# The last head's attention output in two halves: two PSUM banks, matmuls in order of readiness, one half scaled on ScalarE

## The chip, the cores and the metric

The kernel runs on one core of a Trainium2 chip. The metric is the device time of one execution in microseconds (us). The profile's span is the part of it between the first and the last instruction, here 1.7 to 3.0 us shorter, mostly 1.7 to 1.9. A transfer's issue is the instruction that starts it; its landing is the moment when its semaphore reports it complete. In the lines of the profile PE is TensorE, DVE is VectorE, ACT is ScalarE, POOL is GpSimd, and SPq and ACTq are the queues of the sync engine and of ScalarE, which issue the transfers here.

## The reference

Attention with an additive bias, for 4 x 8 heads, 1024 positions and head size 64, all in float32:

```
scores = q @ k^T / sqrt(64) + bias                    # bias [1, 1, 1024, 1024]
attn   = exp(scores - max) / (sum(exp(scores - max)) + 1e-8)
out    = attn @ v
```

## The kernel before

The heads are worked in 16 pairs. Scores are made transposed, 128 keys by 512 queries at a time; one such piece is a **block**, and there are 512 of them. For each block TensorE makes the scores, ScalarE takes the exponential (three blocks an instruction), VectorE multiplies by a table of exp(bias), and TensorE multiplies by V, to which a column of ones is appended, so that the 65th column is the sum of the weights. Eight blocks, one for each 128 keys, add up to the output of one head and 512 queries. They accumulate in one PSUM bank (PSUM is the memory of the tiles `ps_x` and `ps_s` in the code); then VectorE takes the reciprocal of the sums and scales.

The last eight blocks, 504 to 511, belong to the last head's second half of the queries. Blocks 510 and 511 are special: their bias is added in PSUM before the exponential, so they need no multiply. The Python program holds a list scheduler that decides the order of instructions on each engine when the program is built.

```python
    late_bias = {NB - 2: 0, NB - 1: 1}                 # NB = 512
    ...
    def av_bank(b, tag):                               # one block's 4 matmuls with V
        pr, h, qh, kc = banks[b]
        if kc == 0:
            po[h] = ps_x.tile([P, QC, D1], F32, tag=tag, name="po")
        acc = po[h]
        e = e_at(b, 1)
        for i in range(QC):                            # QC = 4 chunks of 128 queries
            nc.tensor.matmul(acc[:, i, :], e[:, 0, i * P:(i + 1) * P], vall[:, 2 * pr + h, kc, :],
                             start=(kc == 0 and i == 0), stop=(kc == NCH - 1), skip_group_check=True)
        if kc < NCH - 1:
            return None
        def evac():
            ...
            nc.vector.reciprocal(rs[:], acc[:, :, D:D1])
            c0 = qh * QC
            if b == NB - 1:                            # the very last one: two scalings, two transfers
                m = QC // 2
                for i, q in ((0, nc.sync), (m, nc.scalar)):
                    nc.vector.tensor_tensor(oall[:, c0 + i:c0 + i + m, :], acc[:, i:i + m, :D],
                                            rs[:, i:i + m, :].to_broadcast([P, m, D]), op=ALU.mult)
                    q.dma_start(out=of[2 * pr + h][:, c0 + i:c0 + i + m, :], in_=oall[:, c0 + i:c0 + i + m, :])
                return
            ...
    # order of the blocks on TensorE, last 16: as numbered
                av_order += list(range(u, NB))
```

The softmax here doesn't subtract the row's maximum and nothing guards it: scores larger than these inputs give would overflow.

Of the kernel before, what the change touches and what calls it, by code (L numbers as in the profile page):

```python
# [8 lines left out]
F32 = mybir.dt.float32  # L9
BF = mybir.dt.bfloat16  # L10
ACTF = mybir.ActivationFunctionType
ALU = mybir.AluOpType
# [3 lines left out]
def kernel(  # L16
# [15 lines left out]
    nc = tc.nc  # L32
    B, H, S, D = q.shape
    P = 128
    NCH = S // P
    D1 = D + 1
    NP = B * H // 2
    scale = 1.0 / (D ** 0.5)
    HQ = S // 2
    QC = NCH // 2  # L40
# [4 lines left out]
    of = out.rearrange("b h (p c) d -> (b h) p c d", p=P)  # L45
# [6 lines left out]
    op = ctx.enter_context(tc.tile_pool(name="op", bufs=2))  # L52
    small = ctx.enter_context(tc.tile_pool(name="small", bufs=4))
    ps_s = ctx.enter_context(tc.tile_pool(name="ps_s", bufs=2, space=bass.MemoryType.PSUM))
    ps_x = ctx.enter_context(tc.tile_pool(name="ps_x", bufs=1, space=bass.MemoryType.PSUM))
# [7 lines left out]
    vall = consts.tile([P, 2 * NP, NCH, D1], BF)  # L63
# [42 lines left out]
    banks = [(pr, h, qh, kc) for pr in range(NP) for qh in range(2) for kc in range(NCH) for h in range(2)]  # L106
    NB = len(banks)
# [8 lines left out]
    def e_at(b, n):  # L116
        if b // ET not in etiles:
            etiles[b // ET] = ep.tile([P, ET, HQ], BF, name="E")
        return etiles[b // ET][:, b % ET:b % ET + n, :]
# [57 lines left out]
    po = {}  # L177

    def av_bank(b, tag):
# [5 lines that stand above are left out]
        for i in range(QC):  # L185
# [6 lines that stand above are left out]
            if qh == 0:  # L192
                oalls[h] = op.tile([P, NCH, D], F32, tag=f"o{h}", name="oall")
            oall = oalls[h]
            rs = small.tile([P, QC, 1], F32, name="rs")
            nc.vector.reciprocal(rs[:], acc[:, :, D:D1])  # L196
            c0 = qh * QC
            if b == NB - 1:

                m = QC // 2  # L200
                for i, q in ((0, nc.sync), (m, nc.scalar)):
                    nc.vector.tensor_tensor(oall[:, c0 + i:c0 + i + m, :], acc[:, i:i + m, :D],
                                            rs[:, i:i + m, :].to_broadcast([P, m, D]), op=ALU.mult)
                    q.dma_start(out=of[2 * pr + h][:, c0 + i:c0 + i + m, :], in_=oall[:, c0 + i:c0 + i + m, :])
                return
            nc.vector.tensor_tensor(oall[:, c0:c0 + QC, :], acc[:, :, :D],  # L206
                                    rs[:].to_broadcast([P, QC, D]), op=ALU.mult)
            if pr == NP - 1:
                nc.sync.dma_start(out=of[2 * pr + h][:, c0:c0 + QC, :], in_=oall[:, c0:c0 + QC, :])
            elif qh == 1:  # L210
                nc.sync.dma_start(out=of[2 * pr + h], in_=oall[:])
        return evac

    with tc.manual_schedule():
# [97 lines left out]
        for u in range(0, NB, 16):  # L312
            if u + 16 < NB:
                av_order += [u + 2 * i for i in range(8)] + [u + 2 * i + 1 for i in range(8)]
            else:
                av_order += list(range(u, NB))
        av_next = 0

        def unit_of(b):
            return banks[b][:3]  # L320
# [44 lines left out]
        def pe_piece():  # L365
            if not pieces:
                return None
            pr, which, half = pieces[0]
            if pr not in raw_at or (pr < NP and pr not in raws):
                return None  # L370
            i = min(len(filled), NO - 1)
            while order[i][0] != "S":
                i -= 1
            at = slots[order[i][1]][0]
            if at < (pr - 2) * 32 + 8:
                return None

            left = NCH - av_next % NCH
            busy = x_unit.get(unit_of(av_order[av_next])) if av_next % NCH else None
            tags = sorted((x_free[x], x) for x in x_free if x != busy)  # L380
            if busy and left < 4 and at < pr * 32 - 16:
                return None
            if not busy and av_next and at < pr * 32 - 16 and tags[0][0] + SEM < t_pe and len(tags) > 1 and tags[1][0] > t_pe:
                return None
            free, tag = tags[0]
            ready = max(free + SEM, raw_at[pr][1 - which])

            def emit(t):
                pieces.pop(0)
                copy = transpose_pe(pr, which, half, tag) if pr < NP else late_bias_pe(tag)  # L390
                cost = COPYK if which else COPYQ
                x_free[tag] = 1e12

                def run(t2):
                    copy()
                    if (pr, which, half) == (0, 1, 1):
                        for x in range(2):
                            for y in range(2):
                                nc.vector.memset(mask[x * D:(x + 1) * D, y, :], 1.0 if x == y else 0.0)
                    x_free[tag] = t2 + cost  # L400
                    piece_end[(pr, which, half)] = t2 + cost
                    if pr < NP and which == 0 and half == 1:
                        if pr + 3 < NP:
                            load_qk(pr + 3)
                            raw_at[pr + 3] = (t2 + 7000, t2 + 7000)
                        if pr + 2 < NP:
                            load_v(pr + 2)
                dve_q.append((t + pe_cost(t, TP) + SEM, 0, cost, run))
            return ready, TP, emit

        def pe_av():
            if av_next >= NB:
                return None
            b = av_order[av_next]
            if b not in mul_at:
                return None
            ready = mul_at[b] + SEM
            u = unit_of(b)
            if banks[b][3] == 0:
                free, tag = min((x_free[x], x) for x in x_free)  # L420
                ready = max(ready, free + SEM)
            else:
                tag = x_unit[u]

            def emit(t):
                nonlocal av_next
                x_unit[u] = tag
                x_free[tag] = 1e12
                evac = av_bank(b, tag)
                av_next += 1  # L430
                if evac:
                    def run(t2):
                        evac()
                        x_free[tag] = t2 + EVAC
                    dve_q.append((t + AV + SEM, 3 if u == (NP - 1, 0, 1) else 1, EVAC, run))
            return ready, AV, emit
# [54 lines left out]
                return None  # L491
            return max(t_act, filled[i] + SEM), cost_act(i), i

        while len(act_end) < NO or av_next < NB or dve_q:
            c = []
            a, d, p = act_pick(), dve_pick(), pe_pick()
            if a:
                c.append((a[0], 0))
            if d:
                c.append((max(t_dve, d[0]), 1))  # L500
            if p:
                c.append((p[0], 2))
            if not c:
                p = pe_pick(force=True)
                c.append((p[0], 2))
            t, who = min(c)
            if who == 0:
                i = a[2]
                item = order[i]
                t_act = t + a[1]  # L510
                act_end.append(t_act)
                if item[0] == "S":
                    s_exp(item[1])
                    for b in slots[item[1]]:
                        exp_at[b] = t_act
                        if b in late_bias:
                            mul_at[b] = t_act
                else:
                    b_exp(item[1], item[2])
                    for kc in range(4):  # L520
                        eb_at[(item[1], item[2] + kc)] = t_act
            elif who == 1:
                if d in dve_q:
                    dve_q.remove(d)
                t_dve = t + d[2]
                d[3](t)
            else:
                t_pe = t + pe_cost(t, p[1])
                p[2](t)
# [30 lines left out]
```

## Time and profile before

| kernel before | |
|---|---|
| time, median of 6 runs | 251.45 us (250.32 to 252.20) |
| span of the profiled run | 249.37 us |
| ScalarE busy | 239.1 us, 96% of the span |
| start of the last-but-one multiply | 243.49 us |
| issue of the last output transfer | 246.28 us |

What the change can touch begins with the last-but-one multiply of VectorE, so I call its start **T** and give the times of the tail from T. They are taken from the trace's records, which are in nanoseconds. The lines of the page and of the tail are shown with the prediction.

### The profile page before, as it was taken

How to read it: one execution, taken by the hardware profiler on the slowest of the kernel's cores; microseconds unless marked ns; L12 is line 12 of the kernel's file. 1: busy time of each engine (PE TensorE's matmuls, PEld its weight loads, DVE VectorE, ACT ScalarE, POOL GpSimd, SP SyncE). 2: the span in 40 equal slices, each digit the busy share in tenths (PEclk: the TensorE clock that was granted, in tenths of full speed). 3: DMA queues.
4: the chain of work that ended last, by engine and by line, in shares of the span. 5: the costliest groups of instructions: out<-in, count | busy, mean ns of one | idle time of the engine just before them, and what ended most of it. 6: DMA issues, size and time to landing. Idle time of an engine off the chain costs nothing.

```text
span 249.4 us, 7121 instructions
## 1 busy us (share of the span) xinstructions
PE 228.1 (91%) x3096; PEld 141.6 (57%) x3151; DVE 220.5 (88%) x384; ACT 239.1 (96%) x181; POOL 52.6 (21%) x72
## 2 busy tenths in 40 slices
PE   6869999999999999999999999999999999999893
PEld 2346656656655655556566555566565555665552
DVE  3619799999999999999999999999999999988884
ACT  3799999999999999999999999999999999999991
POOL 6562315303113132204150130416000000000000
PEclk9999999999999999999999999999999999999998
DMA  8899999942923986923957194939901102020112
GB/s 145 171 206 184 192 122 164 122 94 45 169 45 71 108 112 113 113 87 49 165 82 89 47 117 93 121 95 113 111 34 43 45 0 88 3 84 3 63 45 64
DMA packets 48175, 23.79 MB, mean 95 GB/s; under 512 B 34448, under 2 KB 44048, under 8 KB 47888
## 3 DMA queue, kind: packets, MB, share of 16 engines
q0 software_dynamic: 42272, 14.42, 53.1%
q1 hardware_dynamic: 5312, 8.59, 9.6%
q8 instruction: 24, 0.39, 0.6%
q10 hardware_dynamic: 560, 0.33, 0.5%
q14 instruction: 7, 0.06, 0.1%
HBM read 29.36 MB, written 8.39 MB: 151 GB/s over the span
## 4 chain that ended last, share of the span: by engine, by line
ACT 82%; PE 10%; DVE 3%; issue 2%; DMA 2%; SPq 0%; DVEq 0%; ACTq 0%
ACT E L136 79%; PE ps L129 7%; ACT eb L149 3%; PE po L186 2%; DMA q0f<-in_q_dram 2%; PE px L89 1%; DVE E L161 1%; DVE E L155 1%; DVE oall L206 0%; DVE qT L98 0%; PE pq L250 0%; DVE rs L196 0%; PE px L245 0%; SPq L216 0%; ACT qr L260 0%
## 5 line engine op out<-in xcount | busy, mean ns | idle before, releaser
L136 ACT ACTIVATE E<-ps 128x1536 bf16<-128x1536 f32 (+2 forms) x172 | 230.1, 1681 | 2.0 <-PE ps L129 1.9
L129 PE MATMUL ps<-qT,kT 128*128 128x512 bf16 x457 | 135.3, 381 | 11.3 <-ACT E L136 4.8
L186 PEld LDWEIGHTS <-E 128*128 128x128 bf16 x2048 | 83.2, 98 | 38.8 <-DVE E L158 2.2
L158 DVE TENSOR_TENSOR E<-E,eb 128x2048 bf16<-128x2048 bf16 x78 | 94.1, 1217 | 7.6 <-ACT eb L149 6.4
L186 PE MATMUL po<-vall,E 128*128 128x65 bf16 x2048 | 92.9, 194 | 1.8 <-DVE E L158 0.5
L129 PEld LDWEIGHTS <-kT 128*128 128x128 bf16 x512 | 45.6, 97 | 43.1 <-issue 8.1
L161 DVE TENSOR_TENSOR E<-E,eb 128x1024 bf16<-128x1024 bf16 x92 | 61.0, 682 | 0.9 <-ACT E L136 0.7
L81 POOL DMA_DIRECT2D vall<-in_v_dram x32 | 28.1, 883 | 8.2 <-DVE vall L277 3.9
L75 POOL DMA_DIRECT2D kr<-in_k_dram x15 | 10.5, 700 | 87.6 <-PE px L89 86.3
L206 DVE TENSOR_TENSOR oall<-po,rs 128x256 f32<-128x256 f32 x63 | 26.7, 424 | 2.2
L98 DVE TENSOR_TENSOR qT<-px,mask 128x1024 bf16<-128x1024 bf16 x31 | 21.3, 687 | 2.8 <-PE px L89 1.9
L76 POOL DMA_DIRECT2D qr<-in_q_dram x15 | 10.8, 717 | 25.0 <-PE px L89 23.8
L102 DVE COPY kT<-px 128x512 bf16<-128x512 bf16 x31 | 13.1, 421 | 3.2 <-PE px L89 3.1
L196 DVE RECIPROCAL rs<-po 128x4 f32<-128x4 f32 x64 | 11.3, 176 | 2.6 <-PE po L186 2.2
L89 PE MATMUL px<-ident,qr 128*64 128x128 bf16 x248 | 12.8, 225 | 0.1
L89 PE MATMUL px<-ident,kr 128*64 128x128 bf16 x248 | 12.8, 224 | 0.1
L89 PEld LDWEIGHTS <-qr 128*64 128x64 bf16 x248 | 7.9, 109 | 8.6 <-issue 8.1
L89 PEld LDWEIGHTS <-kr 128*64 128x64 bf16 x248 | 7.9, 109 | 5.6 <-issue 3.6
L149 ACT ACTIVATE eb<-pb 128x2048 bf16<-128x2048 bf16 x4 | 7.5, 1878 | 0.0
L144 PE MATMUL pb<-ident,btraw 128*128 128x128 bf16 x64 | 4.6, 225 | 1.7 <-ACT eb L149 1.2
L144 PEld LDWEIGHTS <-btraw 128*128 128x128 bf16 x64 | 4.5, 147 | 2.5 <-issue 2.2
L155 DVE TENSOR_TENSOR E<-E,eb 128x1024 bf16<-128x1024 bf16 (+1 forms) x6 | 4.6, 774 | 0.6 <-ACT E L136 0.6
(41 smaller groups left out, 21.0 us busy)
## 6 DMA issues: line engine op xcount, KB each, us to landing
out_dram<-oall SPq DMA_DIRECT2D x30, 256.0 KB, 2.0
vall<-in_v_dram POOLq DMA_DIRECT2D x32, 128.0 KB, 5.8
kr<-in_k_dram POOLq DMA_DIRECT2D x15, 256.0 KB, 3.9
qr<-in_q_dram POOLq DMA_DIRECT2D x15, 256.0 KB, 4.5
btraw<-in_bias_dram POOLq DMA_DIRECT2D x2, 1024.0 KB, 10.9
out_dram<-oall SPq DMA_DIRECT2D x3, 128.0 KB, 1.7
q0f<-in_q_dram ACTq DMA_DIRECT2D x1, 128.0 KB, 2.5
k0f<-in_k_dram SPq DMA_DIRECT2D x1, 128.0 KB, 2.8
```

The source lines that it names most:

```text
L81: nc.gpsimd.dma_start(out=vall[:, 2 * pr + t, :, :D], in_=vf[pr, :, t])
L89: nc.tensor.transpose(px[t * D:(t + 1) * D, c, :], src[:, t, half * QC + c, :], ident[:])
L98: nc.vector.tensor_tensor(dst[:, :, half * HQ:(half + 1) * HQ], px.rearrange("p c q -> p (c q)").unsqueeze(1).to_broadcast([P, 2, HQ]), ma ...
L102: nc.vector.tensor_copy(dst[:, half * QC:(half + 1) * QC, :], px[:])
L129: nc.tensor.matmul(ps[:, j, :], kT[:, kc, :], qT[:, h, qh * HQ:(qh + 1) * HQ], start=True, stop=b not in late_bias)
L136: nc.scalar.activation(e_at(slots[g][0], n), open_ps.pop(("S", g))[:, :n, :], ACTF.Exp, scale=scale)
L149: nc.scalar.activation(eb[:, qh, k0:k0 + 4, :], open_ps.pop(("B", qh, k0))[:, :4, :], ACTF.Exp)
L158: nc.vector.tensor_tensor(e, e, eb[:, qh, kc:kc + 2, :].unsqueeze(2).to_broadcast([P, 2, 2, HQ]), op=ALU.mult)
L161: nc.vector.tensor_tensor(e, e, eb[:, qh, kc:kc + 1, :].to_broadcast([P, n, HQ]), op=ALU.mult)
L186: nc.tensor.matmul(acc[:, i, :], e[:, 0, i * P:(i + 1) * P], vall[:, 2 * pr + h, kc, :], start=(kc == 0 and i == 0), stop=(kc == NCH - 1), ...
L196: nc.vector.reciprocal(rs[:], acc[:, :, D:D1])
L206: nc.vector.tensor_tensor(oall[:, c0:c0 + QC, :], acc[:, :, :D], rs[:].to_broadcast([P, QC, D]), op=ALU.mult)
```

## The change

Its intent is a shorter tail. The last head's four chunks are split into two halves of two. Each half has a PSUM bank of its own, so that ScalarE, idle by then, can scale half 0 while VectorE scales half 1. And TensorE takes the blocks in order of readiness: 510 and 511, which need no multiply, go before 508 and 509.

```diff
+    def av_last(x, bs, tag):                       # half x, blocks bs
+        ...
+            po[x] = (ps_x if tag != "s" else ps_s).tile([P, M, D1], F32, tag=tag, name="po")
+        for i in range(M):                         # M = QC // 2 = 2
+            for b in bs:
+                nc.tensor.matmul(acc[:, i, :], e_at(b, 1)[:, 0, (x * M + i) * P:(x * M + i + 1) * P],
+                                 vall[:, 2 * NP - 1, banks[b][3], :], start=..., stop=..., skip_group_check=True)
+        ...
+            nc.vector.reciprocal(rs[:], acc[:, :, D:D1])
+            q = (nc.scalar, nc.sync)[x]
+            if x == 0:
+                for i in range(M):
+                    nc.scalar.activation(oh[:, i, :], acc[:, i, :D], ACTF.Copy, scale=rs[:, i, :])
+            else:
+                nc.vector.tensor_tensor(oh[:], acc[:, :, :D], rs[:].to_broadcast([P, M, D]), op=ALU.mult)
+            q.dma_start(out=of[2 * NP - 1][:, QC + x * M:QC + (x + 1) * M, :], in_=oh[:])
...
-                av_order += list(range(u, NB))
+                av_order += list(range(u, NB - 8))
...
+        def pe_last():                             # scheduler: of both halves, the step that is ready first;
+            ...                                    # 508 and 509 together, and last
```

More of the change, by code (lines that the diff above doesn't have):

```diff
@@ L197, in evac @@
             c0 = qh * QC
-            if b == NB - 1:
-                m = QC // 2
-                for i, q in ((0, nc.sync), (m, nc.scalar)):
-                    nc.vector.tensor_tensor(oall[:, c0 + i:c0 + i + m, :], acc[:, i:i + m, :D],
-                                            rs[:, i:i + m, :].to_broadcast([P, m, D]), op=ALU.mult)
-                    q.dma_start(out=of[2 * pr + h][:, c0 + i:c0 + i + m, :], in_=oall[:, c0 + i:c0 + i + m, :])
-                return
             nc.vector.tensor_tensor(oall[:, c0:c0 + QC, :], acc[:, :, :D],
@@ L211, in evac @@
                 nc.sync.dma_start(out=of[2 * pr + h], in_=oall[:])
+        return evac
+    M = QC // 2
+    last_left = [list(range(NB - 8, NB)) for _ in range(2)]
+    def av_last(x, bs, tag):
+        first = len(last_left[x]) == 8
+        if first:
+            po[x] = (ps_x if tag != "s" else ps_s).tile([P, M, D1], F32, tag=tag, name="po")
+        acc = po[x]
+        for b in bs:
+            last_left[x].remove(b)
+        for i in range(M):
+            for b in bs:
+                nc.tensor.matmul(acc[:, i, :], e_at(b, 1)[:, 0, (x * M + i) * P:(x * M + i + 1) * P],
+                                 vall[:, 2 * NP - 1, banks[b][3], :], start=first and i == 0 and b == bs[0],
+                                 stop=not last_left[x] and b == bs[-1], skip_group_check=True)
+        if last_left[x]:
+            return None
+        def evac():
+            oh = small.tile([P, M, D], F32, name=f"oh{x}")
+            rs = small.tile([P, M, 1], F32, name=f"rh{x}")
+            nc.vector.reciprocal(rs[:], acc[:, :, D:D1])
[6 more added lines that the diff above has]
+            q.dma_start(out=of[2 * NP - 1][:, QC + x * M:QC + (x + 1) * M, :], in_=oh[:])
         return evac
@@ L315 @@
             else:
-                av_order += list(range(u, NB))
+                av_order += list(range(u, NB - 8))
         av_next = 0
+        NA = len(av_order)
         def unit_of(b):
@@ L378, in pe_piece @@
             left = NCH - av_next % NCH
-            busy = x_unit.get(unit_of(av_order[av_next])) if av_next % NCH else None
+            busy = x_unit.get(unit_of(av_order[av_next])) if av_next < NA and av_next % NCH else None
             tags = sorted((x_free[x], x) for x in x_free if x != busy)
@@ L409, in pe_piece, with emit @@
             return ready, TP, emit
+        last_tag = [None, None]
+        def pe_last():
+            best = None
+            for x in range(2):
+                left = last_left[x]
+                if not left or (x == 1 and last_tag[0] is None):
+                    continue
+                steps = [[b] for b in left if b not in (NB - 4, NB - 3)] or [[NB - 4, NB - 3]]
+                for bs in steps:
+                    if any(b not in mul_at for b in bs):
+                        continue
+                    ready = max(mul_at[b] for b in bs) + SEM
+                    tag = last_tag[x]
+                    if tag is None and x == 0:
+                        free, tag = min((x_free[y], y) for y in x_free)
+                        ready = max(ready, free + SEM)
+                    elif tag is None:
+                        if len(act_end) < NO - 1 or len(filled) < NO:
+                            continue
+                        tag = "s"
+                        ready = max(ready, act_end[NO - 2] + SEM)
+                    c = (max(ready, t_pe), x, bs, tag)
+                    if best is None or c[0] < best[0]:
+                        best = c
+            if best is None:
+                return None
+            ready, x, bs, tag = best
+            cost = len(bs) * AV // 2
+            def emit(t):
+                if last_tag[x] is None and x == 0:
+                    x_free[tag] = 1e12
+                last_tag[x] = tag
+                evac = av_last(x, bs, tag)
+                if evac:
+                    dve_q.append((t + cost + SEM, 1, EVAC, lambda t2: evac()))
+            return ready, cost, emit
         def pe_av():
-            if av_next >= NB:
-                return None
+            if av_next >= NA:
+                return pe_last()
             b = av_order[av_next]
@@ L492, in act_pick @@
             return max(t_act, filled[i] + SEM), cost_act(i), i
-        while len(act_end) < NO or av_next < NB or dve_q:
+        while len(act_end) < NO or av_next < NA or any(last_left) or dve_q:
             c = []
```

## The prediction

> **What bounds the kernel now.** I read the page's engine shares first, then the chain that ended last for the whole span and again for its last few microseconds, and then the timeline of those microseconds, because the diff touches nothing earlier.
>
> ```profile
> PE 228.1 (91%) x3096; PEld 141.6 (57%) x3151; DVE 220.5 (88%) x384; ACT 239.1 (96%) x181; POOL 52.6 (21%) x72
> ACT 82%; PE 10%; DVE 3%; issue 2%; DMA 2%; SPq 0%; DVEq 0%; ACTq 0%
> ```
>
> ScalarE's exponentials set the pace: 239.1 of 249.4 us busy and 82% of the chain. The change adds and removes no exponential. What it can move is the tail behind the last one. The chain for 243 us to the end:
>
> ```profile
> 242.11 1.35 ACT E L136
> 243.47 0.02 issue
> 243.49 1.31 DVE E L155 x2
> 244.79 0.05 issue
> 244.84 0.68 PE po L186 x16
> 245.52 0.02 issue
> 245.54 0.19 DVE rs L196
> 245.74 0.02 issue
> 245.76 0.29 DVE oall L202
> 246.05 0.20 DVEq L555
> ```
>
> So the tail hangs not on the last exponential but on the one before it: that ends at 243.47, then two multiplies with the bias table run on VectorE (banks 506/507, then 508/509 of the 512 score blocks), then 16 matmuls, a reciprocal and the scaling. The timeline gives the neighbours:
>
> ```profile
> 243.22 1.15 ACT L136 ACTIVATE E<-ps 128x1024 bf16<-128x1024 f32 x1
> 244.24 0.42 PE L186 MATMUL po<-vall,E 128*128 128x65 bf16 x8 [0.19 <-DVE E L155]
> 244.70 0.17 DVE L196 RECIPROCAL rs<-po 128x4 f32<-128x4 f32 x1
> 244.84 0.67 PE L186 MATMUL po<-vall,E 128*128 128x65 bf16 x16 [0.18 <-DVE E L155]
> 244.91 0.42 DVE L206 TENSOR_TENSOR oall<-po,rs 128x256 f32<-128x256 f32 x1
> 245.54 0.18 DVE L196 RECIPROCAL rs<-po 128x4 f32<-128x4 f32 x1 [0.21 <-PE po L186]
> 245.76 0.49 DVE L202 TENSOR_TENSOR oall<-po,rs 128x128 f32<-128x128 f32 x2
> 246.08 0.33 SPq L204 DMA_DIRECT2D out_dram<-oall  x1
> 246.28 0.36 ACTq L204 DMA_DIRECT2D out_dram<-oall  x1
> ```
>
> Three things are to be seen. The last exponential (two blocks, 510 and 511, which get no multiply because their bias was added before) ends at 243.22 + 1.15 = 244.37, 0.47 us before the 16 matmuls start at 244.84: eight of the 16 wait only because the program order puts them behind 508/509. VectorE still has the other head's scaling in hand from 244.70 to 245.33. And ScalarE is idle from 244.37. The last output transfer is issued at 246.28; the span ends 3.1 us later, at 249.4.
>
> **What the Trainium skill says.** "ScalarE: Activation LUTs", section "What ACT_TABLE_LOAD costs": an ACTIVATE with immediate scale and bias takes 186 ns plus 0.833 ns a column, a per-partition pointer operand adds about 93 ns, and two in a row overlap by about 93 ns; a switch of table set costs about 2.66 us. The trace agrees with the first: a 128-column cast on ScalarE took 298 ns, the formula gives 293. Same page, "Table sets: the hidden batching unit": copy is in every set. The trace fits this without proving it: it has one ACT_TABLE_LOAD (1283 ns), and the cast and copy rows at its start needed no other, but they are not ACTIVATE rows. "PSUM — Partial Sum Buffer", section "PSUM bank collisions raise a hardware error": two engines may not access one bank in the same partitions at once. That is why the halves need two banks before ScalarE and VectorE may scale them side by side; no row of this trace shows it. "Perfetto Trace Analysis", section "DMA Instruction — HWDGE (DVE, Sync)": the row of such a transfer covers its issue alone, not the data. The trace agrees: rows of 0.33 and 0.36 us, landing after 1.6 us.
>
> **The change part by part.**
>
> *Order and number of matmuls.* The last head keeps 32 matmuls (8 blocks x 4 chunks before, 2 halves x 8 blocks x 2 chunks after), so PE's work is the same. I walked the program's own list scheduler by hand from the state it has when block 504 comes up; before that nothing differs. In pairs of matmuls, the order comes out as 504, 505 of half 0, 504 of half 1, 506, 507 of half 0, 505 of half 1, 510, 511 of half 0, 506, 507, 510 of half 1, then the four of 508/509 of half 0, then 511 and 508/509 of half 1. The 16 matmuls from 244.84 to 245.51 start over 0.67 - 0.20 = 0.47 us when the last one's own 0.20 us (mean 194 ns in the page) is taken off: about 0.032 us each. The 16 from block 506 of half 0 to block 510 of half 1 can start at 244.24 and need 16 x 0.032 = 0.51 us, so they are through at 244.75, before the multiply of 508/509 lets anything more start at 244.84. Only 10 matmuls are then left, not 16. Half 0 starts its fourth at 244.84 + 3 x 0.032 = 244.94 and is complete at about 245.13; half 1 starts its last at 244.84 + 9 x 0.032 = 245.13 and is complete at about 245.33. Before, all was complete at 245.52: gains of 0.39 and 0.19 us **on PE**.
>
> *VectorE in between.* The other head's scaling is still queued first, until 245.33. The next instruction there starts up to 0.08 us before the last one's end (245.97 against 245.76 + 0.29 = 246.05), so half 0's reciprocal starts at about 245.26, not at 245.15, and ends, at 0.17 us, about 245.43. Half 1's reciprocal runs about 245.40 to 245.57, its one scaling (128x128, 0.28 us in the present rows) 245.61 to 245.89, and its transfer is issued on the SP queue at about 245.92 (before: 246.08).
>
> *ScalarE.* Two added activations of 64 columns: by the page 186 + 93 + 53 = 332 ns (an estimate), the second 332 - 93 = 239 ns later. From 245.45 they end at 246.02, and the transfer goes out on ScalarE's queue at about 246.05 (before: 246.28). This half is now **the later one**, so it sets the end: 246.28 - 246.05 = 0.23 us gained.
>
> *Removed and unmoved.* One of two 0.28 us scalings leaves VectorE, one reciprocal of 0.17 us joins; the transfers stay two of 64 KB with 1.6 us to landing, and the 3.1 us behind the last issue stay. Half 1's bank is taken from the score buffers, free once the next-to-last exponential ends at 243.47; its first matmul comes in PE's order at about 243.9, so no wait.
>
> Sum: span 249.4 - 0.23 = 249.2; time 251.31 - 0.2 = 251.1 us.
>
> **The rivals.** *Nothing gained:* VectorE, not PE, is the bound of the tail. Its queue (multiply, other head's scaling, two reciprocals, one scaling) has hardly become shorter, and if its reciprocals start only when the other head's scaling is wholly through and ScalarE's activations take 0.4 us each (as the 256-column cast did, 0.40), the last issue comes at 246.25: time 251.3. For it: the 0.42 us row at 244.91. Against: VectorE idled 0.21 us before the reciprocal at 245.54, and that idle time goes. *Full gain:* if the rivals for VectorE were absent, half 0's 0.39 us would come through: 250.9. Against it is that same row. *A table switch:* if an activation of kind copy made the set be loaded again, some 2.6 us would stand on the path: 253.8. Against: the single load at the start. *A wait for PSUM in half 1, or a changed order upstream:* some tenths longer, 251.6; the scheduler's branch for earlier blocks is untouched.
>
> **Range and chances.** The runs before spread from 250.32 to 251.62, more than the whole effect, so the range is that of the runs shifted by my 0.2: 250.2 to 251.8. Over 2% is 5 us; everything from the last exponential's end to the last issue is 246.28 - 244.37 = 1.9 us, so faster by 2% is out of reach even if all that vanished; 0.5% is left for surprise. Slower by 2% needs twice a table switch: 1%. Within 2%: 98.5%.
>
> **What would show it.** In the new profile: 10 matmuls after the multiply of 508/509, not 16; the reciprocal of half 0 directly behind the other head's scaling with no idle time on VectorE; two activations of about 0.33 us; the last issue on ScalarE's queue 0.2 us earlier against the last multiply's end; still one table load. A last issue at or behind 1.45 us after that multiply (now 246.28 - 244.78 = 1.50) makes the gain wrong; a second table load, or idle PE before half 1's first matmul, makes the mechanism wrong.

## More of the kernel before

Beside them, two lines on the start matter later, the landing of the bias (page, part 6: size, then median us from issue to landing) and ScalarE's third bias exponential (timeline of ScalarE: start, duration):

```profile
btraw<-in_bias_dram POOLq DMA_DIRECT2D x2, 1024.0 KB, 10.9
```

```profile
24.87 1.88 ACT L149 ACTIVATE eb<-pb 128x2048 bf16<-128x2048 bf16 x1
```

There is no idle time in brackets behind the second line: ScalarE did not wait there.

## The result

The changed kernel took 251.59 us (median of 6, 251.34 to 251.82), the one before 251.45 us (median of 6, 250.32 to 252.20). The ratio is 1.0011, with a 95% interval of 0.9987 to 1.0035: the same. (A ratio is the mean time of one kernel's runs over that of the other's of the same rounds, so it is not quite the ratio of the medians.) The span of the profiled run was 249.76 us, 0.4 us *longer*.

The timeline of the tail after the change (start, duration, engine, line, operation; in brackets idle time before and what ended it):

```profile
243.99 1.29 DVE L155 TENSOR_TENSOR E<-E,eb 128x1024 bf16<-128x1024 bf16 x2 [0.31 <-ACT E L136]
244.74 1.09 PE L219 MATMUL po<-vall,E 128*128 128x65 bf16 x26 [0.25 <-DVE E L155]
245.20 0.18 DVE L196 RECIPROCAL rs<-po 128x4 f32<-128x4 f32 x1
245.41 0.42 DVE L198 TENSOR_TENSOR oall<-po,rs 128x256 f32<-128x256 f32 x1
245.75 0.28 DVE L228 RECIPROCAL rh<-po 128x2 f32<-128x2 f32 x2
245.95 0.52 ACT L232 ACTIVATE oh<-po,rh 128x64 f32<-128x64 f32 x2 [1.07 <-DVE rh L228]
246.07 0.29 DVE L234 TENSOR_TENSOR oh<-po,rh 128x128 f32<-128x128 f32 x1
246.39 0.33 SPq L235 DMA_DIRECT2D out_dram<-oh  x1
246.50 0.36 ACTq L235 DMA_DIRECT2D out_dram<-oh  x1
```

This trace is half a microsecond late before the tail begins: T is 243.99 here and was 243.49. Measured from T, the tail did become shorter: last issue at 246.50 - 243.99 = 2.51 us, before at 2.79. VectorE has no idle time left between the other head's scaling (245.41) and the reciprocals, and ScalarE and VectorE scale side by side.

The half microsecond came from elsewhere. The same two lines of the start as shown of before:

```profile
btraw<-in_bias_dram POOLq DMA_DIRECT2D x2, 1024.0 KB, 12.1
```

```profile
25.37 1.88 ACT L149 ACTIVATE eb<-pb 128x2048 bf16<-128x2048 bf16 x1 [0.57 <-PE pb L144]
```

In this run the bias landed later and ScalarE stood still for 0.57 us at 25 us. No instruction there was changed. So there were two questions: is that chance, and how much of the 0.28 us at the last issue reaches the end?

For the second, the records give this, in us from T:

| | last issue | last landing | end of the span |
|---|---|---|---|
| before | 2.789 | 4.401 | 5.879 |
| after | 2.505 | 4.196 | 5.769 |
| gained | 0.284 | 0.205 | 0.110 |

Of 0.284 us, 0.079 was lost between issue and landing and 0.095 between landing and end.

### The profile page after: what moved, and what is told of

It is laid out like the page before. It is cut to its first block, busy times and chain, and to the rows that moved or that the text cites. A ratio compares the mean times of both kernels' runs of the same rounds, so it can differ in the third digit from the quotient of the medians.

```text
span 249.8 us, 7178 instructions
## 1 busy us (share of the span) xinstructions
PE 231.1 (93%) x3151; PEld 141.7 (57%) x3151; DVE 220.3 (88%) x384; ACT 239.7 (96%) x183; POOL 52.6 (21%) x72
## 4 chain that ended last, share of the span: by engine, by line
ACT 72%; PE 15%; DMA 7%; issue 2%; DVE 2%; POOL 1%; SPq 0%; ACTq 0%
ACT E L136 70%; PE ps L129 9%; DMA btraw<-in_bias_dram 5%; PE po L186 3%; PE px L89 2%; DMA q0f<-in_q_dram 1%; ACT eb L149 1%; POOL vall L81 1%; DVE E L155 1%; PE pb L144 0%; DVE E L161 0%; DVE oall L198 0%; DVE qT L98 0%; PE pq L274 0%; SPq L240 0%
## 5 line engine op out<-in xcount | busy, mean ns | idle before, releaser
L129 PE MATMUL ps<-qT,kT 128*128 128x512 bf16 x512 | 139.3, 380 | 8.7 <-ACT E L136 4.8
L186 PEld LDWEIGHTS <-E 128*128 128x128 bf16 x2016 | 82.0, 97 | 38.4 <-DVE E L158 2.2
L186 PE MATMUL po<-vall,E 128*128 128x65 bf16 x2016 | 91.5, 194 | 1.2 <-DVE E L158 0.5
```

Of the source, the lines that this page charges most:

```text
L129: nc.tensor.matmul(ps[:, j, :], kT[:, kc, :], qT[:, h, qh * HQ:(qh + 1) * HQ], start=True, stop=b not in late_bias)
```

## The experiments

My theory: (1) the total time is blurred by a start that varies by chance; (2) from T on, the change gains what the table shows, the loss between issue and landing coming from the other transfers and the loss after it from the order in which the program's end waits for its transfers. The rivals: the change costs something upstream; or one part of it does all the work and the others none. Twelve kernels ran. Every timed ratio to the kernel before was "same"; the tail from T repeats within some 30 ns (before: end at 5.879 and, in quiet_before, 5.865; after: 5.769, 5.742, 5.745).

### quiet_before and quiet_after: is it the bias load?

```diff
-        for at, x in ((5, (0, 0)), (7, (0, 4)), (11, (1, 0)), (13, (1, 4))):
+        for at, x in ((5, (0, 0)), (7, (0, 4)), (13, (1, 0)), (15, (1, 4))):
```

The same edit was made in both kernels; the order of the last instructions on TensorE and VectorE stayed as it was.

> The kernel before, with two of the bias-table steps put two exponentials later, so that a late landing of the second bias load can no longer hold up ScalarE. Theory (the 0.5 us by which the changed kernel was behind at 243 us is the chance of when that load lands, seen as 0.57 us idle before the third bias exponential): no idle time before any of the four bias exponentials, runs spread over less than 0.6 us (before: 250.32 to 252.20), median about 250.9. Rival (the 0.5 us was made by the change): the spread stays as wide. The tail keeps its shape: last issue 2.79 us after the start of the last-but-one multiply, end of the span 5.88 us after it.

> The changed kernel with the same two steps put later. Theory: no idle time before the bias exponentials; last issue 2.51 us after the start of the last-but-one multiply (0.28 less than before the change), end of the span 5.77 us after it (0.11 less only: 0.08 lost between issue and landing, 0.10 lost in the end-of-program waits); median 0.1 us under quiet_before. Rival (the change costs something upstream that eats its gain): as slow as quiet_before or slower, though the tail is shorter.

The tails came as expected (last issue 2.791 and 2.505, end 5.865 and 5.742), and no bias exponential waited. But the runs spread as widely as ever: 249.96 to 251.80 and 249.87 to 252.42 (medians 251.25 and 251.02; ratios to before 1.0009 and 1.0006, neither clear of 1). My guess at the **source** of the spread was wrong. The profiles show where most of it is. Here is ScalarE's timeline at the start of two of the kernels below, first order_only, then order_shift:

```profile
6.32 0.60 ACT L136 ACTIVATE E<-ps 128x512 bf16<-128x512 f32 x1 [0.66 <-PE ps L129]
7.21 6.39 ACT L136 ACTIVATE E<-ps 128x1024 bf16<-128x1024 f32 x5 [0.29 <-PE ps L129]
```

```profile
6.01 0.60 ACT L136 ACTIVATE E<-ps 128x512 bf16<-128x512 f32 x1 [1.10 <-PE ps L129]
7.43 1.02 ACT L136 ACTIVATE E<-ps 128x1024 bf16<-128x1024 f32 x1 [0.83 <-PE ps L129]
8.71 1.45 ACT L136 ACTIVATE E<-ps 128x1536 bf16<-128x1536 f32 x1 [0.26 <-PE ps L129]
11.03 2.79 ACT L136 ACTIVATE E<-ps 128x1536 bf16<-128x1536 f32 x2 [0.87 <-PE ps L129]
```

Up to the fourth exponential ScalarE waits for scores (the brackets) two to four times here, not for the same length in each run; the fourth starts at 11.03 us in the second view and, by the records, at 9.46 in the first. From there to T it is 232.90 to 232.93 us in thirteen of the fourteen profiles, whichever kernel; the fourteenth is the first profile of the changed kernel, with 233.58, which is the late bias load. So a span is the sum of a start of 9.5 to 11.1 us, a middle that is constant, and a tail that belongs to the kernel. The measured time has one more part that varies: what lies outside the span. In most timed runs it is 1.7 to 1.9 us, but it goes up to 2.97 in the slowest run of order_only (252.87 us with a span of 249.9) and to 2.42 in that of quiet_after (252.42 with 250.0); no run here shows why. The rival "it costs something upstream" falls: the middle is the same with and without the change. Which of the start's input loads makes ScalarE wait I did not separate.

### order_only: the order alone

One bank, one reciprocal, two VectorE scalings, as before; only 510 and 511 go ahead of 508 and 509 (on the base of quiet_before):

```diff
-                av_order += list(range(u, NB))
+                av_order += list(range(u, NB - 4)) + [NB - 2, NB - 1, NB - 4, NB - 3]
...
-            if b == NB - 1:
+            if b == NB - 3:                            # and the start of the evacuation likewise
```

> quiet_before with nothing of the change but the order: one bank, one reciprocal, two VectorE scalings as before, but the last head's blocks 510 and 511 go before 508 and 509. Theory 1 (the reordering alone carries the gain, since VectorE is busy with the other head's scaling until then): 8 matmuls after the last multiply, last head's reciprocal starts about 1.77 us after the last-but-one multiply's start in place of 2.06, last issue about 2.50, as good as the whole change. Theory 2 (two banks and ScalarE carry most of it): last issue at 2.7 or later.

The tail in its timeline (T is 242.37):

```profile
243.12 1.02 PE L186 MATMUL po<-vall,E 128*128 128x65 bf16 x24 [0.19 <-DVE E L155]
243.79 0.42 DVE L206 TENSOR_TENSOR oall<-po,rs 128x256 f32<-128x256 f32 x1
244.18 0.18 DVE L196 RECIPROCAL rs<-po 128x4 f32<-128x4 f32 x1
244.39 0.49 DVE L202 TENSOR_TENSOR oall<-po,rs 128x128 f32<-128x128 f32 x2
244.71 0.34 SPq L204 DMA_DIRECT2D out_dram<-oall  x1
244.91 0.36 ACTq L204 DMA_DIRECT2D out_dram<-oall  x1
```

TensorE now does the 24 matmuls in one piece, without the second wait it had before, and the reciprocal follows right behind the other head's scaling. The last issue came at 2.545, the last landing at 4.150, the end at 5.623. That is **0.12 us better than the whole change** (5.742) and 0.24 better than before. Theory 1 of the expectation stands: the reordering carries the gain. But of the 0.12 us only 0.03 is an earlier landing (4.150, against 4.184 in quiet_after), no more than the tail's own blur; the rest comes behind the landing (1.473 us against 1.558), where one wait fewer follows, as rotate shows below. The timed ratio was 1.0014 (0.9983 to 1.0046): the start hides all this.

### vec_both: the whole change without ScalarE

```diff
-            if x == 0:
+            if x == 2:                                 # never: both halves on VectorE
                 for i in range(M):
                     nc.scalar.activation(...)
```

> quiet_after with both halves scaled on VectorE, ScalarE unused. If ScalarE's share is worth what the change intends, the last issue moves from 2.51 to about 2.68 us after the start of the last-but-one multiply (two reciprocals and two scalings in a row on VectorE from 1.76), and the end of the span by 0.1 to 0.2. If ScalarE only takes over what VectorE would do as fast, the last issue stays at 2.5.

The last issue came at 2.674, as expected, 0.17 us later than with ScalarE. But the end came at 5.722, not later than quiet_after's 5.742; here the expectation missed. The last landing was at 4.244, only 0.06 later than quiet_after's 4.184, as the two transfers were now 0.40 us apart and the last one took 1.57 us; and one wait fewer stood behind it at the end. ScalarE's help at the issue is real; 0.06 us of it is left at the landing, and here the one wait fewer outweighs that. (Timed ratio 1.0003, 0.9970 to 1.0036.)

### rotate: the waits at the program's end

The compiled program ends with the sync queue waiting for the eight semaphores of its hardware transfers one after the other. Before the change the transfer that lands last is on the seventh of them, after it on the sixth. One earlier output cut in two moves every later transfer by one semaphore:

```diff
-                nc.sync.dma_start(out=of[2 * pr + h], in_=oall[:])
+                for c in ((0, QC) if (pr, h) == (7, 1) else (None,)):
+                    r = slice(None) if c is None else slice(c, c + QC)
+                    nc.sync.dma_start(out=of[2 * pr + h][:, r, :], in_=oall[:, r, :])
```

> quiet_after with one earlier output cut into two transfers, so that the two last transfers report to the next two of the eight semaphores that the program's end waits for one after the other. All times from the start of the last-but-one multiply. Theory (0.10 us of the gain is lost because, after the change, two waits stand behind the one that comes last, and before it one): last landing stays at 4.19, end of the span 5.66 in place of 5.74 to 5.77. Rival (the loss lies elsewhere): end at 5.74 to 5.77.

The last landing stayed at 4.184, the end moved to 5.681: 0.061 us earlier than quiet_after, a little less than expected. From the last landing to the end it takes 1.56 to 1.57 us where two waits follow (the changed kernel's three profiles), 1.46 to 1.50 where one follows (before, quiet_before, order_only, vec_both, rotate, dose) and 1.42 where none does (order_rotate). Rotate's step is not the wait alone, for the cut also adds a row to the sync queue, and rows matter, as after_shift shows below: rotate took 1.50, the five others with one wait, without the added row, 1.46 to 1.48. The four kernels not listed here come below too.

### no_xfer and no_other: is the other head in the way?

In no_xfer the other head's last transfer is sent early with stale data; in no_other its last reciprocal and scaling are left out too. Both leave part of that head's output wrong. (The check does not see this part.)

```diff
             if pr == NP - 1 and h == 0:
+                if qh == 0:                            # both 128 KB now; nothing at qh == 1
+                    nc.sync.dma_start(out=of[2 * pr][:, :QC, :], in_=oall[:, :QC, :])
+                    nc.sync.dma_start(out=of[2 * pr][:, QC:, :], in_=oall[:, :QC, :])
+            # no_other: also, at the top of evac
+            if (pr, h, qh) == (NP - 1, 0, 1): return
```

> quiet_after, but the other head's last 128 KB go out early with stale data (a wrong result on purpose); its scaling on VectorE stays. Theory A (the last two transfers are held up behind the other head's packets): from the last issue to its landing 1.61 us as before the change, in place of 1.68. Theory B (they hold up each other, being issued 0.11 us apart in place of 0.20): still 1.68, end of the span still 5.74 to 5.77 after the last-but-one multiply's start.

> quiet_after without the other head's last reciprocal, scaling and transfer (a wrong result on purpose). From the start of the last-but-one multiply: if VectorE's queue holds up half 0, its reciprocal starts at about 1.65 in place of 1.76 (as soon as its last matmul is through) and the last issue comes at 2.39 in place of 2.505. If PE is the bound, nothing moves.

In no_xfer the last issue-to-landing took 1.666 us, hardly less than quiet_after's 1.679. Theory A falls, and B is left: the two last transfers hold up each other. Over all profiles this time goes with the distance of the last two issues: 1.74 us at 0.04 us apart (no_other), 1.67 to 1.69 at 0.11, 1.61 to 1.64 at 0.20, 1.57 at 0.40, 1.60 at 0.92. In no_other half 0's reciprocal started at 1.683 in place of 1.762 and the last issue came at 2.437 (expected 1.65 and 2.39), so VectorE's queue does hold up half 0; but the last landing stayed at 4.178. What was gained at the issue was lost again between issue and landing (1.74 us), with the two transfers closer still.

Neither expectation foresaw the end: 5.258 and 5.274, almost 0.5 us earlier than in quiet_after although the landing was the same. I come to that below.

### dose: does the end follow ScalarE's half one for one?

```diff
-                for i in range(M):
+                for i in list(range(M)) * 3:
                     nc.scalar.activation(oh[:, i, :], acc[:, i, :D], ACTF.Copy, scale=rs[:, i, :])
```

> quiet_after with ScalarE's two scalings done three times over: four activations more at 0.21 us. If the half on ScalarE sets the end one for one, the last issue moves by 0.85 to 3.35 us after the start of the last-but-one multiply; with the transfers no longer side by side its landing takes 1.6 and the end of the span comes at 6.44 (by 0.70 later, as 0.07 of contention and 0.10 of end waits are given back). If the end hangs on VectorE's half, it stays at 5.75.

The last issue came at 3.319 and the end at 6.399: 0.81 and 0.66 later than in quiet_after, by the expectation's account (0.08 given back between issue and landing, 0.08 in the waits). The end follows the last landing; it does not hang on VectorE's half.

### after_again and order_rotate

after_again is the changed kernel once more, unedited. order_rotate is order_only with the cut of rotate.

> The changed kernel once more, in the same rounds as the kernel before. From the start of the last-but-one multiply: last issue 2.505, end 5.75 to 5.77. Theory (the whole difference in time beyond the tail is the start of the program, where the input loads land by chance): from the fourth large exponential's start to the last-but-one multiply the two kernels agree within 0.02 us unless the second bias load is late; the ratio to the kernel before lies between 0.997 and 1.003, on either side of 1.

> order_only (the readiness order alone, one bank, VectorE alone) with the earlier output cut in two as in rotate: the candidate for the best version. From the start of the last-but-one multiply: last issue 2.55, landing 4.15, end of the span 5.55, which is 0.32 us before the kernel before and 0.2 before the whole change. In the timed runs this is 0.1% and stays inside the spread that the start of the program makes (some 250 to 252 us).

after_again: last issue 2.501, end 5.745, middle 232.925 (before: 232.920), ratio 1.0002 (0.9980 to 1.0025). order_rotate: last issue 2.541, landing 4.177, end 5.594, ratio 0.9994 (0.9960 to 1.0029). The end is 0.29 us before the kernel before; 0.32 had been expected, the landing being 0.03 later than hoped.

### after_shift and order_shift: the half microsecond of no_xfer

I looked for what no_xfer had changed besides the transfer. The rows of the sync queue differ: it had 82 in the trace, where before, after and most others had 83. In *every* profile that queue stands still for 0.41 to 0.43 us between its 79th and 80th row, counted from the program's start. In before, after and their quiet versions these are two drain rows at the very end, and all engines wait. The sync queue's rows of the end of before, between 248.04 and 248.60 us (duration in ns: min, median, max; first and last start):

```profile
L555 SPq DRAIN  x2: 7/68/130, 248.1 to 248.5; - x2
```

The two drains are 0.4 us apart and one of them takes 130 ns. With one row fewer the pause falls one row later, beside rows of GpSimd for which the end of the program waits in any case (in no_xfer the pause ends at 4.92 us from T, those rows at 5.03). To test this without touching any work, six empty rows were added to the sync queue at the start, where it idles, to the changed kernel (after_shift) and to order_rotate (order_shift):

```diff
         nc.sync.dma_start(out=q0f[1].rearrange("p c d -> p (c d)"), in_=qf[0][:, 1, :QC * D])
+        for _ in range(6):
+            nc.sync.drain()
```

> The changed kernel with six empty drain rows more on the sync queue at the start, nothing else. In all ten runs and both kernels so far that queue stands still for 0.41 to 0.43 us between its 79th and 80th row, counted from the start of the program; where the queue had one row fewer, the end came 0.48 us earlier, whatever else was changed. Theory (the pause goes by the row's number and lies on the path): now it falls into the time in which the queue waits for the other head's transfer; last landing stays at 4.19 after the last-but-one multiply's start, end of the span 5.27 in place of 5.75. Rival (the 0.48 us came from the transfer taken away): end at 5.75.

> order_rotate with the same six rows: readiness order alone, last transfer on the last of the eight semaphores, pause moved. Last landing 4.15 to 4.18, end of the span 5.10 to 5.15 after the last-but-one multiply's start: 0.75 us before the kernel before, 0.64 before the changed kernel. In the timed runs 0.3%, at the edge of what the spread of the start lets be seen.

The same rows of after_shift, between 247.35 and 247.55 us:

```profile
L622 SPq DRAIN  x2: 7/7/7, 247.4 to 247.5; - x2
```

The pause was again behind the 79th row, which is now an earlier wait, and the drains follow each other at once. after_shift: landing 4.190 as always, end **5.225**, 0.52 us earlier than after_again. order_shift: landing 4.176, end **5.095**, 0.78 us before the kernel before (5.879) and 0.65 before the change (5.745). The rival, that the missing transfer had given the half microsecond, falls. Six rows of nothing moved the end about four times as far as the change did (0.52 us against 0.11 to 0.13).

In the timed runs after_shift has 250.50 us and order_shift 250.72, with 250.91 for the kernel before in the same rounds; the ratios are 0.9984 (0.9953 to 1.0015) and 0.9988 (0.9955 to 1.0020). Both lean the right way and neither is clear of 1. order_shift has the shortest tail of all correct versions, and I take it for the best one; its lead in whole-run time is not shown.

## Why the prediction was right, and where it was not

The measured 251.59 us lies in the range of 250.2 to 251.8, and "within 2%" was right. Neither speaks for the predicted gain: the unchanged kernel's 251.45 lies in the range as well, and 2% is 5 us, where the tail gained 0.1. The predicted 251.1 was 0.5 us too low. Point by point, in us from T (the prediction's clock minus 243.49):

- **What bounds the kernel** held: ScalarE's middle did not move, and all of the effect lies behind T.
- **Order and number of matmuls** held: 10 start after the last multiply, from 1.35 to 1.64; half 1 was complete at 1.84, as predicted.
- **VectorE in between** held: half 0's reciprocal started at 1.764 (predicted 1.77), overlapping the end of the other head's scaling, with no idle time.
- **ScalarE** was mis-sized slightly: 0.31 us an activation (predicted 0.332) and 0.21 from one to the next (0.239); the prediction had checked the formula on a cast, not on an activation. The last issue came at 2.505, predicted 2.56; the gain there was 0.284, predicted 0.23. No second table load was made: there is one row of 1283 ns in the new trace too. ScalarE (1.96 to 2.48) and VectorE (2.08 to 2.37) did read their two banks at the same time, and the result was correct; sharing one bank was not tried. The sign that the prediction set for the gain came: the last issue is 1.21 us after the end of the last multiply, against a limit of 1.45 and 1.50 before.
- **"The 3.1 us behind the last issue stay"** is the step that failed. They went from 3.09 (5.879 - 2.789) to 3.26 (5.769 - 2.505). I had moved the end by the gain of the issue. The runs put two things in its place: two transfers issued 0.11 us apart instead of 0.20 land 0.08 later, and the later one is now followed by two waits instead of one, another 0.10. Of 0.28 us, 0.11 arrived.
- **The rivals:** "nothing gained, VectorE's queue bounds the tail" was half right. That queue delays half 0 by 0.08 us (no_other), but freeing it brought nothing at the landing. The table switch and the wait for a PSUM bank did not occur. A rival that I did not name proved the truest: that the order *alone*, with one bank and no ScalarE, does at least as well.
- **The range** was hit by luck. By its own words it is "that of the runs shifted by my 0.2", but 250.32 to 251.62 less 0.2 is 250.1 to 251.4, and 251.59 lies outside that. The thought behind it, that the spread is wider than the effect, was right: the median was on the other side of 251.31 than predicted, and the start's 1.6 us between the earliest and the latest profile is wide enough for that. Nothing in the runs shows the changed kernel to be slower.

What stays open: which input makes the start vary; and what the pause behind the 79th row is. The one packet of the instruction queue in the tail does not coincide with it (in after_again it starts at 5.51, the pause is from 4.45 to 4.88). That packet came 1.1 us earlier when the six rows were added (4.38 in after_shift; 4.31 in order_shift, 5.43 in order_rotate), so it seems to go by the rows as well; that it has to do with the pause is not shown.

## What to carry to other kernels

A shorter chain to the last issue is not yet a shorter program: follow the gain through the landing and through the waits behind it, and compare from a common event in both traces instead of from zero, because a start that varies by 1.6 us, and up to 1.2 us more outside the span, hide a tail that repeats within 30 ns. Try the cheapest part of a change alone first: here the reordering without second bank and second engine landed its last transfer at 4.15 to 4.18 us, the whole change at 4.18 to 4.20, and at the end it gave twice the gain (0.24 us against 0.12), mostly because one wait fewer happened to stand behind its last transfer.

## What the Trainium skill lacked or had wrong

- "ScalarE: Activation LUTs", "What ACT_TABLE_LOAD costs": for 64 columns with one pointer operand its formula gives 332 ns and 239 ns from one to the next; here, reading PSUM, it was 310 ns and 0.21 us (0.20 us in dose). The page does not say from which memory its figures are.
- "DMA: Bandwidth & Descriptors", "Issuing engines are not separate DMA queues", says that transfers of different issuers interleave on the same DMA engines; it lacks what that costs two small ones: 64 KB on each of two queues landed 1.68 us after the later issue at 0.11 us apart, 1.61 at 0.20, 1.74 at 0.04, while the issue rows kept their 0.33 and 0.36 us.
- "Runtime: NRT & Kernel Launch", "Instruction fetch mechanics", speaks of instruction blocks whose crossing is "mostly hidden". Whether that is what happens here is not shown, but no page has it: a pause of 0.41 to 0.43 us behind the sync queue's 79th row in all fourteen profiles. Moved to where it met a wait (after_shift), it let this program end 0.52 us earlier.
- No page has the cost of the waits for transfers at the end of a program: about 0.06 to 0.1 us for each that stands behind the last to land.
